# Decay-mask rows inside the exponent matmul of a two-layer SSD, attention and convolution block

## The chip, the core and the metric

The kernel runs on one core of one Trainium2 chip. Its metric is the device time of one execution in microseconds (us), given as the median of several runs. Five engines work side by side, each through its own list of instructions in a fixed order: TensorE (PE in the tables; its weight loads are PEld), VectorE (DVE), ScalarE (ACT), GpSimd (POOL) and SyncE (SP). They wait for one another through semaphores. ScalarE and SyncE also issue most of the DMA transfers; a DMA issue stands in the same list as the engine's other instructions.

## What is computed

Two layers of a hybrid block act on 1024 latent and 256 context tokens (T = 1280, ten chunks of 128 tokens). Each layer projects the tokens, runs three branches (a bidirectional Mamba-2 scan "SSD" with 16 heads, a windowed attention and a convolution), gates them, and projects back. The change is in the SSD branch. Cut to what matters, one direction of it is:

```
da    = dt * a                                   # per head and token
cs    = cumsum(da within a chunk of 128)
seg   = cs[l] - cs[s]
decay = exp(where(s <= l, seg, -inf))            # 128 x 128 per head
y_diag = (C B^T * decay) @ (x * dt)
states, entering states: a scan over the ten chunks
y = y_diag + C @ entering * exp(cs)
```

The backward direction does the same on reversed tokens, so its mask is the other triangle, and the two results are added.

## The kernel before, in words

The layers run one after the other, each as an SSD section, an attention section and an output section. The instruction order of each engine is not the order of the source: a scheduler with a simulated timeline places every instruction, and parts under `high_priority` are drawn ahead. The large projections (`pj`, 512 or 256 columns at a time, three products per weight tile) fill TensorE between the smaller pieces of the SSD.

In the SSD section the prologue forms dt, da, the running sums `cs`, and `ld`, the logarithm of dt. The kernel needs, per chunk and head, exponents of the form log dt[s] - cs[s] + cs[l], and forms them with a matmul on bf16 numbers, where each float32 value is split into three bf16 parts. Lines 739 to 761 prepare this for two groups of 8 heads: VectorE writes the parts of `cs` and `ld` into `qq` (columns 0 to 95) and GpSimd writes -1 into columns 96 to 127; TensorE transposes `qq` chunk by chunk into PSUM tiles `pr`, ScalarE copies them out as `L`, and one DMA per group writes the 48 rows of `cs` parts to DRAM (`csd`).

`half(i)` handles 4 heads over all chunks, 4 times a layer. Line 852: VectorE fills two tiles `R` (128 partitions, 2 directions, 4 heads, 128 tokens) with a pattern of ones that picks the heads. For each chunk, `diag` (lines 867 to 896) then

- issues two DMAs that put `cs` of the chunk into rows 96 to 98 of `R` (line 872),
- forms `pc` with five matmuls: a 128-wide one, two 64-wide ones, and two 64-wide ones against the identity that add the mask `mask_lt` (-3e38 where a triangle is not wanted); and `pd` with four 64-wide ones, two of which add `mask_gt`,
- takes the exponential of both on ScalarE (`ex`, `eb`), adds the two on GpSimd, multiplies by C B^T on VectorE.

There are 40 such decay blocks in layer 0 (ten chunks, four halves) and 32 in layer 1, whose two context chunks need none: 72 in all. What surrounds them is `visit` (the result of a chunk) and the state update `S`. The PSUM tiles of the SSD section, `sm`, `pr`, `pc` and `pd`, share one ring of four banks.

## Time and profile before

| what | value |
|---|---|
| median of 3 runs | 2413.73 us (2412.1 to 2414.97) |
| the profiled execution, its own time | 2409.47 us |
| its span, first to last instruction | 2407.7 us |
| TensorE busy | 96% of the span |
| VectorE, ScalarE, GpSimd busy | 64%, 41%, 45% |
| mean granted TensorE clock | 0.985 of full speed |

The page gives busy times per engine. A matmul's duration is that of its flight, and several fly at once; what a matmul costs on TensorE is read from the distance between the starts of two neighbours.

### The profile page before, as it was taken

The numbers are of one execution on the slowest core, as the hardware profiler recorded it, in microseconds if no ns is written. First come the engines' busy times: TensorE is split into PE (matmuls) and PEld (weight loads), VectorE is DVE, ScalarE is ACT, GpSimd is POOL, SyncE is SP. The second block draws the span as 40 slices with busy tenths as digits, with TensorE's granted clock in tenths as the row PEclk, the third lists the DMA queues.
The fourth block names the chain that finished last, engine by engine and source line by source line (L and its number), as shares of the span: only waits on it lengthen the run. The fifth ranks groups of instructions, "written<-read, shape, count | busy, mean of one in ns | idle before, by whom it ended". The sixth has DMA issues, their size and how long they took to land.

```text
span 2407.7 us, 37133 instructions
## 1 busy us (share of the span) xinstructions
PE 2307.0 (96%) x13453; PEld 1817.5 (75%) x13453; DVE 1533.2 (64%) x2738; ACT 979.0 (41%) x2123; POOL 1085.7 (45%) x1249
## 2 busy tenths in 40 slices
PE   6999999999999999999999999999999999999998
PEld 3787678777877776776888788768768676776798
DVE  4679899941276855865354679979423864865634
ACT  6543243422235454444243443343322355463433
POOL 3237663764453222343233337667575531332333
PEclk8999999999999999999999999999999999999999
DMA  7412212233133112248465311111212312235663
GB/s 225 154 58 87 87 49 64 85 100 111 36 90 105 62 38 70 80 141 264 136 185 168 92 40 45 41 41 43 78 54 62 106 48 67 80 97 171 197 179 107
DMA packets 324248, 237.07 MB, mean 98 GB/s; under 512 B 56066, under 2 KB 280546, under 8 KB 324064
## 3 DMA queue, kind: packets, MB, share of 16 engines
q1 hardware_dynamic: 280832, 193.28, 27.2%
q10 hardware_dynamic: 42336, 41.06, 5.5%
q8 instruction: 106, 1.74, 0.3%
q0 software_dynamic: 896, 0.35, 0.1%
q14 instruction: 78, 0.64, 0.1%
HBM read 181.63 MB, written 53.00 MB: 97 GB/s over the span
## 4 chain that ended last, share of the span: by engine, by line
PE 77%; DVE 9%; DMA 5%; POOL 3%; issue 2%; ACT 2%; SPq 1%; ACTq 0%; DVEq 0%; POOLq 0%
PE pj L96 53%; PE sm L96 6%; PE s L96 4%; PE o L96 3%; PE pt L1086 3%; PE po L96 2%; DVE us L508 2%; DMA raw<-oT 1%; PE pc L96 1%; PE pm L96 1%; DMA wm<-w_mod 1%; POOL ex L893 1%; PE rb L96 1%; DVE acc L596 1%; PE sm L912 1%
## 5 line engine op out<-in xcount | busy, mean ns | idle before, releaser
L96 PE MATMUL pj<-hh,wh 128*128 128x512 f32 (+1 forms) x1840 | 692.7, 377 | 7.8 <-ACT wh L416 2.3
L96 PE MATMUL pj<-hl,wh 128*128 128x512 f32 (+1 forms) x1840 | 686.5, 373 | 1.7 <-POOL hl L199 1.7
L96 PE MATMUL pj<-hh,wl 128*128 128x512 f32 (+1 forms) x1840 | 686.4, 373 | 1.7 <-POOL wl L418 1.6
L418 POOL TENSOR_TENSOR wl<-wr,wh 128x512 fp32r<-128x512 f32 x268 | 362.1, 1354 | 516.8 <-ACT wh L416 482.1
L96 PEld LDWEIGHTS pj<-hh,wh 128*128 128x128 f32 x1840 | 350.0, 190 | 70.7 <-issue 6.8
L96 PEld LDWEIGHTS pj<-hh,wl 128*128 128x128 f32 x1840 | 349.5, 190 | 61.3 <-issue 5.0
L96 PEld LDWEIGHTS pj<-hl,wh 128*128 128x128 f32 x1840 | 350.2, 190 | 59.3 <-issue 5.7
L416 ACT ACTIVATE wh<-wr 128x512 fp32r<-128x512 f32 x344 | 215.6, 630 | 365.5 <-PE pj L96 280.2
L508 DVE SCALAR_TENSOR_TENSOR ua<-gl,vec,ua 128x512 f32<-128x512 f32 (+1 forms) x435 | 303.5, 698 | 12.3 <-ACT ua L506 5.7
L596 DVE SCALAR_TENSOR_TENSOR acc<-raw,vec,acc 128x514 f32<-128x514 f32 (+2 forms) x280 | 191.0, 695 | 21.9 <-ACT acc L593 20.3
L96 PE MATMUL pj<-ho,wh 128*128 128x256 f32 (+1 forms) x896 | 180.3, 300 | 1.0 <-ACT wh L416 1.0
L96 PE MATMUL pj<-hx,wh 128*128 128x512 f32 x512 | 163.7, 400 | 6.9 <-DVE hx L500 2.9
L96 PEld LDWEIGHTS pj<-ho,wh 128*128 128x128 f32 x896 | 145.2, 193 | 6.4 <-ACT wh L416 1.2
L893 POOL TENSOR_TENSOR ex<-ex,eb 64x256 f32<-64x256 f32 x144 | 115.5, 802 | 59.4 <-ACT eb L891 52.4
L933 POOL TENSOR_TENSOR xs<-xk,ws 128x256 f32<-128x256 f32 x144 | 90.7, 641 | 112.0 <-PE sm L96 96.8
L1079 ACT ACTIVATE p<-s,sums 128x512 f32<-128x512 f32 (+1 forms) x144 | 95.5, 663 | 107.7 <-DVE sums L1077 69.4
L1076 DVE TENSOR_REDUCE mx<-s 128x1 f32<-128x512 f32 (+1 forms) x144 | 92.4, 654 | 72.0 <-PE s L96 71.6
L96 PE MATMUL pj<-ho,wl 128*128 128x256 f32 (+1 forms) x448 | 134.6, 301 | 1.1 <-POOL wl L418 0.8
L508 DVE SCALAR_TENSOR_TENSOR us<-gl,vec,us 128x512 f32<-128x512 f32 (+1 forms) x150 | 130.3, 869 | 6.8 <-ACT us L506 4.3
L96 PEld LDWEIGHTS pj<-hx,wh 128*128 128x128 f32 x512 | 97.8, 192 | 30.6 <-DVE hx L500 4.7
L907 POOL TENSOR_TENSOR yp<-yp,ye 128x256 f32<-128x256 f32 x136 | 104.3, 783 | 26.6 <-DVE ye L906 26.1
L1086 PE MATMUL pt<-ident,p 128*128 128x128 f32 x640 | 108.5, 283 | 7.2 <-ACT p L1079 6.5
(325 smaller groups left out, 3951.6 us busy)
## 6 DMA issues: line engine op xcount, KB each, us to landing
wr<-w_in SPq DMA_DIRECT2D x160, 256.0 KB
wr<-w_out SPq DMA_DIRECT2D x114, 256.0 KB
wm<-w_mod SPq DMA_DIRECT2D x64, 256.0 KB
raw<-oT ACTq DMA_DIRECT2D x64, 256.0 KB
wr<-w_out SPq DMA_DIRECT2D x76, 128.0 KB
yT<-yT ACTq DMA_DIRECT2D x72, 128.0 KB
wm<-w_mod SPq DMA_DIRECT2D x16, 512.0 KB
wr<-w_in SPq DMA_DIRECT2D x64, 128.0 KB
```

The lines of the kernel that those rows point to most:

```text
L96: nc.tensor.matmul(o, l, r, start=start, stop=stop)
L416: nc.scalar.activation(out=hi, in_=raw, func=AF.Copy)
L418: low_eng[0].tensor_tensor(out=lo, in0=raw, in1=f32(hi), op=ALU.subtract)
L508: nc.vector.scalar_tensor_tensor(out=u if t == 30 else acc, in0=g[:, t:t + n], scalar=vec2[l][:, t, j:j + 1], in1=acc, op0=ALU.mult, op1=A ...
L596: nc.vector.scalar_tensor_tensor(out=acc, in0=raw[:, i0 + t:i0 + t + n], scalar=v1[:, cw:cw + 1], in1=acc, op0=ALU.mult, op1=ALU.add)
L893: nc.gpsimd.tensor_tensor(out=e[q, :, q], in0=e[q, :, q], in1=eb[q], op=ALU.add)
L907: nc.gpsimd.tensor_tensor(out=y, in0=y, in1=ye, op=ALU.add)
L912: nc.tensor.matmul(ps[:, jj * P:(jj + 1) * P], y[:, jj * P:(jj + 1) * P], ident, start=(jj == 0), stop=False, is_transpose=True)
L933: nc.gpsimd.tensor_tensor(out=h3(xs), in0=xc(c), in1=hb(ws3, c, d), op=ALU.mult)
L1076: nc.vector.tensor_reduce(out=mx, in_=s, axis=mybir.AxisListType.X, op=ALU.min)
L1079: nc.scalar.activation(out=flat(p[:, 0:min(nk, 4), :]), in_=s, func=AF.Exp, scale=-1.0, bias=nm[:, j:j + 1], accum_out=sums[:, 3, j:j + 1])
L1086: nc.tensor.transpose(pt[:, q * P:(q + 1) * P], pr[q][:, i, :], ident)
```

## The change

The masks become part of the matmul that forms the exponents. `L` gets 64 more rows that hold the identity (`id64`), `R` gets 64 more rows that hold the mask, and a third plane, so that one pair of 64-wide matmuls of 512 columns gives all of `pc` and one pair of 256 columns all of `pd`. For the room this takes, `ld` and `cs` are added in float32 before they are split, so `L` needs 48 rows of parts and not 96. The `cs` parts for DRAM get tiles of their own (`qc`, transposed to 72 rows, copied out as `cr`), and `csd` keeps three planes. The constant rows of `R` are written by GpSimd once a layer, and the 48 rows that pick the heads by ScalarE at each half.

```diff
-    csd = [dp.tile([2, 3, 2, 2, 4, T], BF16, ...
+    csd = [dp.tile([2, 3, 2, 3, 4, T], BF16, ...
...
+            nc.vector.tensor_tensor(out=ld, in0=ld, in1=cs, op=ALU.add)
...
             for g in range(2):
+                qc = sp.tile([P, NCH, 72], BF16, tag="xk", name="qc", bufs=7)
+                parts(cs, qc, g)
+                for q, c0 in ((slice(0, 64), 24), (slice(64, P), 0)):
+                    nc.scalar.activation(out=qc[q, :, 48:72], in_=qc[q, :, c0:c0 + 24], func=AF.Copy)
                 qq = sp.tile([P, NCH, P], BF16, tag=("cbs", "btok")[g], name="qq")
-                for c0, t in ((0, cs), (48, ld)):
-                    (four VectorE instructions: three bf16 parts of t)
-                nc.gpsimd.memset(qq[:, :, 96:P], -1.0)
+                parts(ld, qq, g)
+                nc.gpsimd.memset(qq[:, :, 48:64], -1.0)
+                nc.scalar.activation(out=qq[:, :, 64:P], in_=id64 (broadcast), func=AF.Copy)
                 lt = sp.tile([P, T], BF16, tag=f"L{g}", name="L")
                 for b0 in range(0, NCH, 4):
                     nb = min(4, NCH - b0)
                     pr = pp.tile([P, 1024], BF16, tag="sm", name="pr", bufs=NSM)
                     for c in range(b0, b0 + nb):
+                        nc.tensor.transpose(pr[0:72, ...], qc[:, c, :], identb)
+                    cr = sp.tile([72, 512], BF16, tag="ex", name="cr", bufs=2)
+                    nc.scalar.activation(out=cr[:, 0:nb * P], in_=pr[0:72, 0:nb * P], func=AF.Copy)
+                    for v, w in enumerate((0, 2, 1)):
+                        nc.scalar.dma_start(out=csd[l][g][:, :, v]..., in_=cr[24 * w:24 * w + 24, 0:nb * P])
+                    pr = pp.tile([P, 1024], BF16, tag="sm", name="pr", bufs=NSM)
+                    for c in range(b0, b0 + nb):
                         nc.tensor.transpose(pr[...], qq[:, c, :], identb)
                     nc.scalar.activation(out=lt[...], in_=pr[:, 0:nb * P], func=AF.Copy)
-                nc.scalar.dma_start(out=csd[l][g]..., in_=lt[0:48, :])
...
+            for _ in range(2):
+                R = sp.tile([P, 3, 4, P], BF16, tag="R", name="R", bufs=2)
+                nc.gpsimd.memset(R[32:64], 0.0)
+                nc.gpsimd.memset(R[64:P, 0:2], 0.0)
+                for v, t0, m in ((0, 0, mask_lt), (1, 64, mask_lt), (2, 0, mask_gt), (2, 64, mask_gt)):
+                    nc.gpsimd.tensor_copy(out=R[64:P, v, :, t0:t0 + 64], in_=m[64:P, 64:P] (broadcast))
... in half(i):
-                for _ in range(2):
-                    R = sp.tile([P, 2, 4, P], BF16, tag="R", name="R", bufs=2)
-                    nc.vector.tensor_copy(out=R, in_=sel4(sel_c) (broadcast))
+                for R in Rs:
+                    for v, d, t0, t1 in ((0, 0, 0, P), (2, 1, 0, P), (1, 1, 0, 64), (1, 0, 64, P)):
+                        nc.scalar.activation(out=R[0:48, v, :, t0:t1], in_=sel_c[0:48, d, ...] (broadcast), func=AF.Copy)
... in diag(c):
-                    for dd in range(2):
-                        nc.scalar.dma_start(out=R[96:99, dd], in_=csd[l][g, :, dd, hf, :, c * P:(c + 1) * P])
+                    nc.scalar.dma_start(out=R[48:51], in_=csd[l][g, :, hf, :, :, c * P:(c + 1) * P])
-                    mm(pc[:, :, qs[1]], lt[0:99, c * P:(c + 1) * P], r0[:, :, qs[1]], start=True, stop=False)
-                    mm(pc[qs[0], :, qs[0]], ll[0], r0[:, :, qs[0]], start=False, stop=False)
-                    mm(pc[qs[1], :, qs[0]], ll[1], r1[:, :, qs[0]], start=False, stop=False)
-                    for q in qs:
-                        mm(pc[q, :, q], identb[:, q], mask_lt (broadcast), start=False, stop=True)
+                    for v, (q, lq) in enumerate(zip(qs, ll)):
+                        mm(pc[q], lq, R[:, v])
...
                     for q, lq in zip(qs, ll):
-                        mm(pc[q], lq, r1[:, :, q], start=True, stop=False)
-                    for q in qs:
-                        mm(pc[q], identb[:, q], mask_gt (broadcast), start=False, stop=True)
+                        mm(pc[q], lq, R[:, 2, :, q])
```

How this moves instructions. On TensorE, at the first decay block of layer 0, the order before was (`sm<-S,ct` and `sm<-xs,btok` are the state products ahead of it; a pair is two matmuls of 64 output rows, `64x4x64` means 64 rows and 256 columns):

```order
L96 MATMUL sm<-S,ct 128x256 x2
L96 MATMUL sm<-xs,btok 128x256 x2
L96 LDWEIGHTS L
L96 MATMUL pc<-R,L 128x4x64
L96 LDWEIGHTS L
L96 MATMUL pc<-R,L 64x4x64
L96 LDWEIGHTS L
L96 MATMUL pc<-R,L 64x4x64
L96 LDWEIGHTS identb
L96 MATMUL pc<-mask_lt,identb 64x4x64
```

On TensorE, at the same place, the order now is the whole block and the projection behind it:

```order
L96 MATMUL sm<-S,ct 128x256 x2
L96 MATMUL sm<-xs,btok 128x256 x2
L96 LDWEIGHTS L
L96 MATMUL pc<-R,L 64x512
L96 LDWEIGHTS L
L96 MATMUL pc<-R,L 64x512
L96 LDWEIGHTS L
L96 MATMUL pd<-R,L 64x4x64
L96 LDWEIGHTS L
L96 MATMUL pd<-R,L 64x4x64
L96 MATMUL pj<-hh_982,wl 128x512
```

Nine matmuls with nine weight loads (a mask matmul and four of `pd` follow the piece above) have become four with four.

On ScalarE, in the set-up of layer 0 where `L` is copied out of PSUM, the order before was (L760 writes `cs` to DRAM, L872 loads it into `R`, `btok` is the next user of the PSUM ring):

```order
L759 ACTIVATE L<-pr 128x512 x2
L759 ACTIVATE L<-pr 128x256
L759 ACTIVATE L<-pr 128x512
L760 DMA cs_104<-L 48x1280
L872 DMA R<-cs_104 3x4x128 x4
L759 ACTIVATE L<-pr 128x512
L759 ACTIVATE L<-pr 128x256
L814 ACTIVATE btok<-sm 128x512
```

On ScalarE, at the same place, the order now is (L772 copies `cr`, L778 `L`, L774 writes to DRAM, L894 loads `R`):

```order
L778 ACTIVATE L<-pr 128x512
L774 DMA cs_107<-cr 6x4x512 x5
L894 DMA R<-cs_107 3x12x128 x2
L774 DMA cs_107<-cr 6x4x512
L772 ACTIVATE cr<-pr 72x256
L778 ACTIVATE L<-pr 128x256
L778 ACTIVATE L<-pr 128x512
L774 DMA cs_107<-cr 6x4x256 x3
L772 ACTIVATE cr<-pr 72x512
L778 ACTIVATE L<-pr 128x512
L774 DMA cs_107<-cr 6x4x512 x3
L772 ACTIVATE cr<-pr 72x512
```

The load of `R`, which waits for a write to DRAM, now stands ahead of two thirds of the copies out of the PSUM ring, and more writes stand between these; `btok` comes after two more rows.

On ScalarE, at the end of the second half in layer 0, the order now is (L902 and L907 are the exponentials `ex` and `eb` of the last blocks, L876 the refill of `R` for the next half, L932 and L933 the result of a chunk):

```order
L876 ACTIVATE R<-sel_c 48x512
L902 ACTIVATE ex<-pc 128x512
L933 DMA yT_105<-yT 128x2x128
L876 ACTIVATE R<-sel_c 48x4x64 x2
L932 ACTIVATE yT<-sm 128x256
L907 ACTIVATE eb<-pd 128x256
L876 ACTIVATE R<-sel_c 48x512
L894 DMA R<-cs_107 3x12x128
```

The refill stands between the exponentials of the last blocks; before, none of it was on ScalarE.

## Rows read from the trace of the kernel before

**Rows 1.** The page, busy time, share of the span and instructions of each engine.

```profile
PE 2307.0 (96%) x13453; PEld 1817.5 (75%) x13453; DVE 1533.2 (64%) x2738; ACT 979.0 (41%) x2123; POOL 1085.7 (45%) x1249
```

**Rows 2.** Windows: stretch, length, busy us (count) per engine, granted clock, DMA, GB/s.

```profile
120.00:580.00 460.00, 448.77 (x2867) 347.28 (x2866) 357.61 (x635) 163.25 (x345) 275.55 (x400) 1.00 0.26 76
1560.00:1600.00 40.00, 32.45 (x211) 22.27 (x210) 34.64 (x59) 14.57 (x32) 34.15 (x47) 0.96 0.12 35
1600.00:1785.00 185.00, 185.00 (x997) 147.89 (x994) 104.63 (x165) 58.59 (x119) 115.51 (x165) 1.00 0.22 58
1785.00:1807.00 22.00, 16.51 (x143) 10.06 (x141) 8.63 (x17) 7.78 (x20) 16.56 (x22) 1.00 0.16 44
```

**Rows 3.** Timeline of PE over one decay block: start, length, line, operation, count.

```profile
177.82 0.42 PE L912 MATMUL sm<-ident,yp 128*128 128x128 f32 x2
178.08 0.51 PE L96 MATMUL pc<-R,L 99*128 99x256 bf16 x3
178.41 0.28 PE L96 MATMUL pc<-mask_lt,identb 128*64 128x256 bf16 x2
178.53 0.28 PE L96 MATMUL pd<-R,L 99*64 99x256 bf16 x2
178.64 0.28 PE L96 MATMUL pd<-mask_gt,identb 128*64 128x256 bf16 x2
178.85 0.33 PE L912 MATMUL sm<-ident,yp 128*128 128x128 f32 x1
```

**Rows 4.** Timeline of the weight loads over the same block.

```profile
178.31 0.11 PEld L96 LDWEIGHTS <-identb 128*64 128x64 bf16 x2
```

**Rows 5.** Timeline of PE, a block with projections between `pc` and `pd`.

```profile
335.69 0.28 PE L96 MATMUL pc<-mask_lt,identb 128*64 128x256 bf16 x2
335.89 0.50 PE L96 MATMUL pj<-hh,wh 128*128 128x512 f32 x1
336.23 0.39 PE L96 MATMUL pj<-hl,wh 128*128 128x512 f32 x1
336.46 0.40 PE L96 MATMUL pj<-hh,wl 128*128 128x512 f32 x1
```

**Rows 6.** Timeline of PE in the set-up of layer 0.

```profile
149.31 0.95 PE L758 MATMUL pr<-identb,qq 128*128 128x128 bf16 x14
150.09 0.50 PE L96 MATMUL pj<-hh,wh 128*128 128x512 f32 x1
...
155.09 1.04 PE L813 MATMUL sm<-ident,raw 128*128 128x128 f32 x8
```

**Rows 7.** Timeline of ACT there; ACTq is its queue issuing DMAs.

```profile
149.93 1.85 ACT L759 ACTIVATE L<-pr 128x512 bf16<-128x512 bf16 x4
151.32 0.36 ACTq L760 DMA_DIRECT2D cs<-L  x1
153.38 1.43 ACTq L872 DMA_DIRECT2D R<-cs  x4
...
155.94 0.60 ACT L814 ACTIVATE btok<-sm 128x512 f32<-128x512 f32 x1
```

**Rows 8.** Timeline of DVE there, two rows of the splitting of `cs`.

```profile
144.04 0.31 DVE L737 TENSOR_SCALAR cs<-cs 128x320 f32<-128x320 f32 x1
...
148.94 0.55 DVE L751 TENSOR_TENSOR qq<-cs,qq 128x160 bf16<-128x160 f32 x2
```

**Rows 9.** Group of line 852 by form: busy us, mean ns, idle before.

```profile
L852 DVE COPY R<-sel_c 128x1024 bf16<-128x1024 bf16 x16 | 14.2, 895 | 3.6 <-PE pd L96 3.4
```

**Rows 10.** The instructions of line 759, durations in ns min/median/max.

```profile
L759 ACT ACTIVATE L<-pr x12: 378/594/628, 149.9 to 1413.2; 128x512 bf16<-128x512 bf16 x8, 128x256 bf16<-128x256 bf16 x4
```

**Rows 11.** Timeline of POOL at the start of layer 0's SSD section.

```profile
62.68 0.66 POOL L752 MEMSET qq<- 128x320 bf16 x2
67.07 1.30 POOL L418 TENSOR_TENSOR wl<-wr,wh 128x512 fp32r<-128x512 f32 x1 [3.72 <-ACT wh L416]
86.22 1.27 POOL L199 TENSOR_TENSOR hl<-xs,hh 128x512 fp32r<-128x512 f32 x1 [17.85 <-ACT xs L198]
```

**Rows 12.** Timeline of PE, first use of that `wl`.

```profile
73.20 0.28 PE L96 MATMUL pj<-hh,wl 128*128 128x256 f32 x1
```

More of the change, by code (lines that the diff above doesn't have):

```diff
@@ L119, in build @@
     nc.vector.tensor_scalar(out=mask_gt, in0=tril, scalar1=-1.0, scalar2=-NEG, op0=ALU.add, op1=ALU.mult)
-    sel_c = cp.tile([P, 16], BF16, name="sel_c")
+    sel_c = cp.tile([P, 2, 8], BF16, name="sel_c")
     sel4 = cp.tile([P, 32], F32, name="sel4")
-    nc.vector.tensor_reduce(out=sel4[:, 0:16], in_=ident[:, 0:96].rearrange("p (a b) -> p b a", b=16), axis=mybir.AxisListType.X, op=ALU.add)
-    nc.vector.tensor_copy(out=sel_c, in_=sel4[:, 0:16])
+    for d in range(2):
+        nc.vector.tensor_reduce(out=sel4[:, 8 * d:8 * d + 8], in_=ident[:, 24 * d:24 * d + 24].rearrange("p (a b) -> p b a", b=8), axis=mybir.AxisListType.X, op=ALU.add)
+    nc.vector.tensor_copy(out=sel_c, in_=sel4[:, 0:16].rearrange("p (a b) -> p a b", b=8))
+    id64 = cp.tile([P, 64], BF16, name="id64")
+    nc.vector.tensor_tensor(out=id64, in0=identb[:, 0:64], in1=identb[:, 64:P], op=ALU.add)
     nc.vector.tensor_reduce(out=sel4, in_=ident.rearrange("p (a b) -> p b a", b=32), axis=mybir.AxisListType.X, op=ALU.add)
@@ L138, in build @@
     yTd = [dp.tile([P, KD, T], F32, name=f"yT{l}") for l in range(DEPTH)]
-    csd = [dp.tile([2, 3, 2, 2, 4, T], BF16, name=f"cs{l}") for l in range(DEPTH)]
+    csd = [dp.tile([2, 3, 2, 3, 4, T], BF16, name=f"cs{l}") for l in range(DEPTH)]
     glTd = [dp.tile([P, 4, RA], F32, name=f"glT{l}") for l in range(DEPTH)]
@@ L737, in ssd_section, with v4, parts @@
             nc.vector.tensor_scalar_mul(out=cs, in0=cs, scalar1=-1.0)
+            nc.vector.tensor_tensor(out=ld, in0=ld, in1=cs, op=ALU.add)
             L = []
+            def v4(ap):
+                return ap.rearrange("p c (d j) -> p c d j", d=2)
+            def parts(t, q, g):
+                x = v4(v3(t))[:, :, :, 8 * g:8 * g + 8]
+                q = [q[:, :, 0:48].rearrange("p c (d a j) -> p c d a j", d=2, a=3)[:, :, :, k, :] for k in range(3)]
+                nc.vector.tensor_copy(out=q[0], in_=x)
+                nc.vector.tensor_tensor(out=x, in0=x, in1=q[0], op=ALU.subtract)
+                nc.vector.tensor_copy(out=q[1], in_=x)
+                nc.vector.tensor_tensor(out=q[2], in0=x, in1=q[1], op=ALU.subtract)
             for g in range(2):
+                qc = sp.tile([P, NCH, 72], BF16, tag="xk", name="qc", bufs=7)
+                parts(cs, qc, g)
+                for q, c0 in ((slice(0, 64), 24), (slice(64, P), 0)):
+                    nc.scalar.activation(out=qc[q, :, 48:72], in_=qc[q, :, c0:c0 + 24], func=AF.Copy)
                 qq = sp.tile([P, NCH, P], BF16, tag=("cbs", "btok")[g], name="qq")
-                def v4(ap):
-                    return ap.rearrange("p c (d j) -> p c d j", d=2)
-                for c0, t in ((0, cs), (48, ld)):
-                    x = v4(v3(t))[:, :, :, 8 * g:8 * g + 8]
-                    q = [v4(qq[:, :, c0 + 16 * k:c0 + 16 * k + 16]) for k in range(3)]
-                    nc.vector.tensor_copy(out=q[0], in_=x)
-                    nc.vector.tensor_tensor(out=x, in0=x, in1=q[0], op=ALU.subtract)
-                    nc.vector.tensor_copy(out=q[1], in_=x)
-                    nc.vector.tensor_tensor(out=q[2], in0=x, in1=q[1], op=ALU.subtract)
-                nc.gpsimd.memset(qq[:, :, 96:P], -1.0)
+                parts(ld, qq, g)
+                nc.gpsimd.memset(qq[:, :, 48:64], -1.0)
+                nc.scalar.activation(out=qq[:, :, 64:P], in_=id64.unsqueeze(1).to_broadcast([P, NCH, 64]), func=AF.Copy)
                 lt = sp.tile([P, T], BF16, tag=f"L{g}", name="L")
@@ L845, in half @@
                 lt = L[g]
[L847 to L853 removed]
+                for R in Rs:
+                    for v, d, t0, t1 in ((0, 0, 0, P), (2, 1, 0, P), (1, 1, 0, 64), (1, 0, 64, P)):
+                        nc.scalar.activation(out=R[0:48, v, :, t0:t1], in_=sel_c[0:48, d, 4 * hf:4 * hf + 4].unsqueeze(2).to_broadcast([48, 4, t1 - t0]), func=AF.Copy)
                 def xc(c):
@@ L870, in diag @@
                     nv[0] += 1
[L871 to L874 removed]
+                    nc.scalar.dma_start(out=R[48:51], in_=csd[l][g, :, hf, :, :, c * P:(c + 1) * P])
                     qs = [slice(0, 64), slice(64, P)]
[L876 removed]
+                    ll = [lt[:, c * P + a:c * P + a + 64] for a in (0, 64)]
                     pc = pp.tile([P, 4, P], F32, tag="sm", name="pc", bufs=NSM)
[L878 to L882 removed]
+                    for v, (q, lq) in enumerate(zip(qs, ll)):
+                        mm(pc[q], lq, R[:, v])
                     e = sp.tile([P, 4, P], F32, tag="ex", name="ex", bufs=2)
@@ L886, in diag @@
                     for q, lq in zip(qs, ll):
-                        mm(pc[q], lq, r1[:, :, q], start=True, stop=False)
-                    for q in qs:
-                        mm(pc[q], identb[:, q], mask_gt[:, q].unsqueeze(1).to_broadcast([P, 4, 64]), start=False, stop=True)
+                        mm(pc[q], lq, R[:, 2, :, q])
                     eb = sp.tile([P, 4, 64], F32, tag="eb", name="eb", bufs=2)
```

14 lines of the change are left out of this document (5 added, 9 removed).

## Prediction

> **What bounds the kernel now.** I read four views in turn. The page's busy line [rows 1] shows TensorE busy for 96% of the span and no other engine above 64%. The table of windows [rows 2] tells where that is strict: in 120 to 580 us TensorE is busy 448.77 of 460 and in 1600 to 1785 all of 185, at a granted clock of 1.00, while VectorE, GpSimd and ScalarE idle for much of the time. In 1560 to 1600 and in 1785 to 1807 TensorE is busy only 32.45 of 40 and 16.51 of 22, and VectorE (34.64) or GpSimd (34.15, 16.56) is as busy as TensorE: there the chain through the engines sets the time. So time taken from TensorE counts in full in the dense stretches, and work given to another engine costs only where TensorE ends up waiting for it. The timeline of single instructions then prices one decay block [rows 3, 5] and the set-up of the exponents [rows 6 to 8, 11, 12].
>
> A matmul's length in the timeline is its flight; its cost is the distance to the next start.
>
> **The decay block.** Before, a block runs from 178.08 to 178.85, 0.77 us [rows 3]. It is five slots of 256 columns (the 128-wide matmul; the 64-wide pair; the mask pair; the `pd` pair; its mask pair), since two 64-wide matmuls lie side by side in one slot. A slot is 0.115: 178.41, 178.53, 178.64. Five are 0.57, and I put the other 0.20 down to two changes between full-width and half-width matmuls, 0.10 each. Now there is a pair of 512 columns and a pair of 256. A start-to-start of 512 columns is 0.23 (336.23 to 336.46, [rows 5]), so 0.23 + 0.115 + 0.20 = 0.545. That is 0.225 less, and for 72 blocks 16.2 us. Besides, one half-width run now replaces a full-width matmul between half-width ones; counted through TensorE's order, changes beside blocks fall from 209 to 175, 34 x 0.10 = 3.4 (the 0.20 from the last mask pair to the next full-width matmul in [rows 5], less 0.115, shows one). Gross gain 19.6.
>
> Bounds of this: if the 512-column pairs take two slots each way (no side by side), nothing is gained; if the changes cost nothing now, 0.10 x 2 x 72 = 14 more. I take the middle, since pairs of 256 columns do lie side by side.
>
> 14 of the 72 blocks lie in the two chained stretches. Their share, 14 x (19.6 / 72) = 3.8, I count a third: +2.5 (bounds 0 and 3.8).
>
> One point on the weights. The load for the second half-width pair, 0.11 long, starts at 178.31 while the `pc` matmuls are still in flight, and the pairs behind it follow 0.115 apart [rows 3, 4]: loads are hidden, and I take nothing for them. The Trainium skill (TensorE: Matmul & The Clock Gate, The mechanism, under packing small matmuls) says that a weight load overlaps matmuls in flight only when its rows of the array differ; the two pairs share their rows, so by it the loads would be exposed, and the trace of before disagrees.
>
> **The set-up, TensorE.** The parts of `cs` are now transposed by themselves: 40 more transposes. Fourteen take 149.31 to 150.09, 0.056 each [rows 6]: +2.2, in full, as TensorE is dense there.
>
> **The set-up, ScalarE.** This is the term with the widest bounds. ScalarE takes its list in order. A load of `R` waits for the write of `cs` to land in DRAM: before, the write is issued at 151.32 for 0.36 and the load starts at 153.38, about 1.7 after the issue's end [rows 7]. In the new order the load stands ahead of two thirds of the copies that empty the PSUM ring. Ahead of `btok` (155.94 in [rows 7]) I count: five copies `cr` at 1.85 / 4 = 0.46, 2.3; eleven more issues at 0.36, 3.9, less 0.7 for two loads of `R` fewer; about 1 where `cr`, with two buffers, waits for its own writes. That is some 6.5 later. TensorE shares the ring of four banks and stalls when it isn't emptied; behind it lie only the transposes `btok` (155.09, [rows 6]). It has 1.1 of the added transposes there to do and I allow 1 of slack, leaving 4. VectorE splits `ld` only after adding `cs`: one add of about 0.31 (as at 144.04, [rows 8]) and the splits of `ld`, now behind those of `cs`, where the last rows ended at 148.94 + 0.55; ScalarE's small copies inside `qc` and of the identity into `qq` stand there too. For this +1. In all +5 for layer 0, bounds 0 (other projections are drawn in) and 8 (everything shows). Layer 1 has more projection matmuls between these transposes, by its order: +1, bounds 0 and 5.
>
> **The refill of R.** VectorE loses 16 fills of 895 ns, 14.2 us [rows 9]; TensorE hardly waits for VectorE in the dense stretches (357.61 of 460, [rows 2]), so 0, with a bound of -3 in the chained ones. ScalarE gets 16 x (2 x 0.594 + 2 x 0.378) = 16 x 1.94 = 31.1 us, by the copies of 512 and 256 columns [rows 10]. ScalarE is busy 163.25 of 460 [rows 2], so it has room, but in a list with fixed order: at each of the six boundaries between halves 3.9 us stand between the exponentials of the last blocks. TensorE has projections to go on with; I take 0.25 a boundary, +1.5 (bounds 0 and 6 x 3.9 = 23). The Trainium skill (ScalarE: Activation LUTs, Rules for kernel authors) wants simple operations on VectorE and not ScalarE, up to about three times as fast in bf16. The rows agree in direction (895 ns for 1024 columns against twice 594 and more), with 14.2 against 31.1 us; on a ScalarE that isn't the bound it makes no time by itself. DMA issues on ScalarE: loads of `R` fall from 144 to 72, writes of `cs` rise from 4 to 36; the loads stand in the dense part, so the exchange favours the blocks slightly, and I take 0.
>
> **GpSimd.** It writes the constant rows of `R` once a layer: per tile memsets of 1536 and 1024 columns, at 0.66 for 640 [rows 11] 2.64, and for both tiles eight copies of 256 that I put at 0.4 each: 8.5 in all with both tiles (bounds 7.3 and 11.7, at 0.26 and 0.8 a copy). Most of it stands ahead of `wl` at 67.07, which has 3.72 idle before it: it comes about 3.9 late (3.3 to 6.7), and is ready near 72.3 for its first use at 73.20 [rows 12]. So 0, bound +2. After it GpSimd has 17.85 idle before 86.22 [rows 11] to catch up.
>
> **The sum.** -19.6 + 2.5 + 2.2 + 5 + 1 + 1.5 = -7.4. The profiled execution's own time is 2409.47, so 2402.1 on its footing; the median of the runs shown is 4.26 above it, and the forecast is 2406.3, put as 2406.
>
> **Rivals.**
>
> A, everything beside the blocks is hidden. TensorE's own balance, -19.6 + 2.2 = -17.4, arrives: 2413.7 - 17.4 = 2396. For it: ScalarE at 35% in the dense stretch, and projections that can be drawn into the set-up. Against: 14 blocks in chained stretches, and the load of `R` placed ahead of the copies.
>
> B, the weights pace the new block. Four loads of 0.11 stand against three slots of 0.115, where before nine stood against five; if those of the `pd` pair can't go while the `pc` pair is in flight, each block pays 0.11, 72 x 0.11 = 7.9: 2406.3 + 7.9 = 2414. Against it is the load at 178.31 [rows 4], which did overlap; for it, that load was of `identb`, and no row shows one of `L` at such a moment. The section of the skill named above is this rival's rule.
>
> C, ScalarE becomes the late engine. If the refills come when the exponentials that release the ring's banks are due, two thirds of 23.3, 15.5, show in place of 1.5: -7.4 - 1.5 + 15.5 = +6.6, 2420. It is slower than before once some 9 of the 23.3 show. For it: one ring of four banks for `pc`, `pd`, `sm` and `pr`, so one late exponential stops TensorE. Against: ScalarE's 300 us idle in 460.
>
> D, the change doesn't do what it says: half-width matmuls of 512 columns don't lie side by side. Then the `pc` pair takes 0.46, 0.23 x 72 = 16.6 more: 2423. Nothing in the rows hints at it but that no half-width pair of 512 is among them.
>
> **How the numbers follow.** A difference under 0.2%, 4.8 us, can't be told from none. Chances: forecast 0.55, A 0.15, B 0.17, C 0.10, D 0.03. Within the forecast the set-up (0 to 8, 0 to 5) and the chained blocks spread it over 2399 to 2412; four fifths of that lies below 2408.9. Faster: 0.44 + 0.15 = 0.59; within: 0.11 + 0.17 = 0.28; slower: 0.13. The range 2394 to 2418 leaves out C and D and a tail of A, under 2 in 10.
>
> **What would show it.** In the profile after: a block's first start to the next full-width start of 0.55, and not 0.66 (B) or 0.77 (D); the start after a 512-column pair 0.23 later. TensorE's busy time lower by about 17, with its idle time in layer 0's set-up higher by some 5: transposes `btok` around 160 less what was saved before them, and a load of `R` in ScalarE's list with idle time before it. Refills between exponentials, with `pc` matmuls waiting for ScalarE by at most a few tenths at a boundary; several us there would be C. `wl` near 71 and its use still at 73. The forecast is wrong if TensorE's idle time grows by more than 17, or if the blocks don't shrink.

## The result and the profile after

The change made the kernel slower. Its median is 2429.86 us (2427.79 to 2434.31), that of the kernel before on the same chip 2414.35 (2412.10 to 2415.70); the ratio is 1.0068, with a 95% interval of 1.0052 to 1.0085. The forecast was 2406, range 2394 to 2418. The profiled execution has a span of 2429.9 us.

The line of busy times, which answers to [rows 1], shows that TensorE is busy for as long as before (2307.0), in a span that is 22 us longer. It has less to do but does it at a lower clock: the mean granted clock is 0.979, where it was 0.985, which leaves out 51 us of full-speed clock instead of 36. Its idle time has grown from 100.7 to 123.1 us.

```profile
PE 2306.8 (95%) x13133; PEld 1812.6 (75%) x13133; DVE 1520.5 (63%) x2726; ACT 1013.5 (42%) x2211; POOL 1091.9 (45%) x1273
```

The span is best cut at points that both kernels pass, at the same projection matmul by count: the set-up of the exponents in layer 0, the rest of layer 0's SSD section with its 40 blocks, and the SSD section of layer 1. The windows of the kernel before (stretch, length, busy us and count of TensorE, its weight loads, VectorE, ScalarE, GpSimd, granted clock, DMA share, GB/s):

```profile
130.90:162.94 32.04, 31.00 (x225) 26.30 (x224) 20.34 (x50) 19.26 (x40) 4.14 (x10) 1.00 0.19 58
162.94:632.21 469.27, 454.08 (x2835) 350.80 (x2834) 341.17 (x595) 154.93 (x326) 285.15 (x402) 0.99 0.28 79
1341.82:1837.93 496.11, 477.57 (x2647) 380.33 (x2646) 354.93 (x588) 184.39 (x366) 291.05 (x402) 0.99 0.19 52
```

and of the changed kernel, from and to the same matmuls:

```profile
135.86:178.02 42.16, 35.26 (x239) 29.02 (x237) 18.64 (x49) 22.40 (x48) 3.23 (x8) 0.92 0.15 47
178.02:640.72 462.70, 444.88 (x2642) 340.33 (x2639) 335.43 (x591) 164.60 (x354) 283.60 (x403) 0.99 0.28 81
1349.28:1859.35 510.07, 480.34 (x2508) 381.60 (x2506) 352.29 (x581) 200.47 (x410) 292.46 (x415) 0.97 0.19 51
```

The set-up takes 10.1 us longer: TensorE idles for 6.9 us where it idled for 1.0, and its clock, which was at the upper of its two levels all through (1.00 is 2.4 GHz), has a mean of 0.92, which over 42.16 us is 3.4 us lost. Layer 0's blocks win 6.6 and layer 1's section loses 14.0. The rest is +5.0 ahead of the set-up (+1.5 in another profile of almost the same program, n2 below, so mostly not the change), -1.0 between the layers and about +1 behind.

The decay block became what the forecast said. The timeline of TensorE at one block, to be held against [rows 3, 5]:

```profile
353.64 0.41 PE L96 MATMUL pc<-R,L 128*64 128x512 bf16 x2
353.88 0.28 PE L96 MATMUL pd<-R,L 128*64 128x256 bf16 x2
354.08 0.50 PE L96 MATMUL pj<-hh,wh 128*128 128x512 f32 x1
354.42 0.39 PE L96 MATMUL pj<-hl,wh 128*128 128x512 f32 x1
```

The 512-column pair lies side by side (0.24 to the next start) and the `pd` pair adds 0.20 with the change of width: 0.44 from the first start to the next full-width start, where it had been 0.77. The other change of width, which lay inside the old block, now lies ahead of it: from the last `sm<-ident,yp` to the block it is 0.20 (median of 11 blocks without a wait) where it was 0.11 (13 blocks). That makes 0.54 in all. The 0.34 behind the block's end is no new cost, since a full-width matmul behind a mask pair showed it too (335.89 to 336.23, [rows 5]). No start is held up by a weight load's 0.11 [rows 4].

The timeline of ScalarE in layer 0's set-up, to be held against [rows 7] (ACTq: its queue issuing DMAs; in brackets idle time and what ended it):

```profile
157.38 1.31 ACTq L774 DMA_DIRECT2D cs<-cr  x1
157.72 0.60 ACT L772 ACTIVATE cr<-pr 72x512 bf16<-72x512 bf16 x1
158.20 0.60 ACT L778 ACTIVATE L<-pr 128x512 bf16<-128x512 bf16 x1
158.73 3.03 ACTq L774 DMA_DIRECT2D cs<-cr  x4
161.94 0.68 ACTq L894 DMA_DIRECT2D R<-cs  x2
162.65 0.71 ACTq L774 DMA_DIRECT2D cs<-cr  x1
163.41 0.38 ACT L772 ACTIVATE cr<-pr 72x256 bf16<-72x256 bf16 x1 [4.61 <-DMA cs<-cr]
163.69 0.37 ACT L778 ACTIVATE L<-pr 128x256 bf16<-128x256 bf16 x1
163.82 0.71 ACTq L774 DMA_DIRECT2D cs<-cr  x1
163.96 0.59 ACT L778 ACTIVATE L<-pr 128x512 bf16<-128x512 bf16 x1
164.57 1.46 ACTq L774 DMA_DIRECT2D cs<-cr  x2
166.15 0.59 ACT L772 ACTIVATE cr<-pr 72x512 bf16<-72x512 bf16 x1 [1.60 <-issue]
166.65 0.58 ACT L778 ACTIVATE L<-pr 128x512 bf16<-128x512 bf16 x1
166.78 2.21 ACTq L774 DMA_DIRECT2D cs<-cr  x3
169.11 0.59 ACT L772 ACTIVATE cr<-pr 72x512 bf16<-72x512 bf16 x1 [1.88 <-issue]
169.61 0.37 ACT L778 ACTIVATE L<-pr 128x256 bf16<-128x256 bf16 x1
169.74 0.71 ACTq L774 DMA_DIRECT2D cs<-cr  x1
169.87 0.59 ACT L841 ACTIVATE btok<-sm 128x512 f32<-128x512 f32 x1
```

A write of `cs` holds ScalarE's list for 0.71 to 0.76 us (3.03 for four; thirteen of them stand ahead of `btok`), twice the 0.36 of [rows 7], and ScalarE copies nothing out of the ring between 158.8 and 163.4 and little until 169.9. The 4.61 us ahead of the copy at 163.41 are filled by seven issues; between the end of the four writes issued in a row (161.76) and the load of `R` (161.94) there is no room for a wait of more than 0.18. TensorE, which has four banks to transpose into, waits. Its longest waits in the set-up, in its own timeline:

```profile
155.46 0.41 PE L770 MATMUL pr<-identb,qc 128*72 128x128 bf16 x4 [1.73 <-ACT qc L760]
163.84 0.38 PE L770 MATMUL pr<-identb,qc 128*72 128x128 bf16 x4 [0.38 <-ACT cr L772]
166.80 0.37 PE L777 MATMUL pr<-identb,qq 128*128 128x128 bf16 x2 [1.93 <-ACT cr L772]
169.76 1.54 PE L840 MATMUL sm<-ident,raw 128*128 128x128 f32 x6 [1.36 <-ACT cr L772]
```

So 3.7 of its 6.9 idle us are waits for the late copies `cr`, and 1.7 one for ScalarE's small copies inside `qc`. With e1 (below) the three waits for `cr` are gone.

GpSimd's constant rows behaved as costed against [rows 11, 12]: the `wl` behind them starts at 71.23 (forecast "near 71") and no TensorE wait hangs on it:

```profile
71.23 1.29 POOL L422 TENSOR_TENSOR wl<-wr,wh 128x512 fp32r<-128x512 f32 x1
```

The refill is 30.8 us of ScalarE, by the groups of its line (31.1 forecast):

```profile
L876 ACT ACTIVATE R<-sel_c 48x512 bf16<-48x512 bf16 x32 | 19.2, 623 | 13.6 <-PE pc L96 12.3 <-POOL R L784 1.3
L876 ACT ACTIVATE R<-sel_c 48x256 bf16<-48x256 bf16 x32 | 11.6, 408 | 0.0
```

### The profile page after: what moved, and what is told of

Read it like the earlier page. It is cut to its first block, busy times and chain, and to the rows that moved or that the text cites. A ratio compares the mean times of both kernels' runs of the same rounds, so it can differ in the third digit from the quotient of the medians.

```text
span 2429.9 us, 36533 instructions
## 1 busy us (share of the span) xinstructions
PE 2306.8 (95%) x13133; PEld 1812.6 (75%) x13133; DVE 1520.5 (63%) x2726; ACT 1013.5 (42%) x2211; POOL 1091.9 (45%) x1273
```

## The experiments

Eighteen kernels were run. Ratios are to the kernel before, run in the same sessions, with 95% intervals; 0.1% is 2.4 us. "Set-up", "layer 0" and "layer 1" are the three windows above, found in each profile by the same matmuls. Since a profile is a single execution, a difference in a window is relied on only where several kernels repeat it. The profiled executions of the kernel before (2409.5 us), of b1 (2401.1) and of e8 (2420.7) lie 4 us or more under the median of their kernel, those of b2 (2410.9) and e7 (2406.7) 4 us or more above theirs.

| kernel | ratio | set-up | layer 0 | layer 1 |
|---|---|---|---|---|
| before | 1 | 32.0 | 469.3 | 496.1 |
| changed | 1.0068 [1.0052, 1.0085] | 42.2 | 462.7 | 510.1 |
| e1 writes on SyncE | 1.0036 [1.0025, 1.0047] | 38.2 | 466.8 | 505.3 |
| e2 fill on VectorE | 1.0041 [1.0027, 1.0056] | 43.7 | 467.5 | 508.6 |
| e4 both | 1.0025 [1.0014, 1.0035] | 38.0 | 463.3 | 506.3 |
| e5 and first loads on SyncE | 0.9994 [0.9985, 1.0004] | 37.4 | 465.1 | 507.8 |
| e6 and one transpose | 0.9992 [0.9980, 1.0003] | 36.7 | 466.7 | 500.4 |
| e7 and refill by DMA | 0.9935 [0.9920, 0.9950] | 36.1 | 455.8 | 501.1 |
| e8 changed, refill by DMA | 1.0048 [1.0035, 1.0061] | 43.5 | 456.7 | 507.1 |
| e3 changed, masks' time again | 1.0084 [1.0069, 1.0099] | 42.2 | 465.2 | 506.7 |
| e9 e7, masks' time again | 1.0016 [1.0007, 1.0025] | 36.8 | 463.0 | 501.0 |
| b2 before, no masks | 0.9959 [0.9945, 0.9973] | 32.1 | 462.0 | 501.4 |
| b1 before, fill on ScalarE | 0.9973 [0.9962, 0.9985] | 31.9 | 464.6 | 497.0 |
| b3 before, refill by DMA | 1.0015 [1.0006, 1.0023] | 31.9 | 469.3 | 501.3 |
| n1 before, other order | 1.0021 [1.0012, 1.0030] | 32.7 | 472.7 | 500.3 |
| n2 changed, other order | 1.0060 [1.0045, 1.0074] | 43.0 | 462.3 | 506.2 |
| n4 e6, other order | 0.9994 [0.9985, 1.0003] | 36.7 | 462.9 | 502.4 |
| n3 e7, other order | 1.0010 [1.0001, 1.0019] | 36.1 | 460.2 | 499.3 |
| n5 e7, nearly the same order | 0.9968 [0.9957, 0.9980] | 36.1 | 455.8 | 498.5 |
| n6 b2, other order | 0.9978 [0.9969, 0.9987] | 32.7 | 460.4 | 501.8 |

**ScalarE's list in the set-up: e1, e2, e4, e5.**

```diff
-  nc.scalar.dma_start(out=csd[l][g][:, :, v]..., in_=cr[24 * w:24 * w + 24, ...])
+  nc.sync.dma_start(out=csd[l][g][:, :, v]..., in_=cr[24 * w:24 * w + 24, ...])      # e1, e4, e5
-  nc.scalar.activation(out=R[0:48, v, :, t0:t1], in_=sel_c..., func=AF.Copy)
+  nc.vector.tensor_copy(out=R[0:48, v, :, t0:t1], in_=sel_c...)                      # e2, e4, e5
-  nc.scalar.dma_start(out=R[48:51], in_=csd[l][g, :, hf, :, :, ...])
+  (nc.sync if i == 0 and nv[0] <= 2 else nc.scalar).dma_start(out=R[48:51], ...)     # e5
```

Expected of e1: 

> The changed kernel with one difference: the writes of the cs parts to DRAM are issued by SyncE and not by ScalarE. In the changed kernel each of them takes 0.71 us in ScalarE's list (the forecast had 0.36), and TensorE lost 10.1 us to the kernel before between 131 and 163 us, and 2.6 in layer 1's set-up. Theory 1 (ScalarE's list holds up the set-up): these two stretches win back most of it, 8 to 12 us, so about 2419. Theory 2 (ScalarE's list is not what holds TensorE there; the transposes and the wait for the write to land are): within 3 us of the changed kernel's 2430. Theory 3 (the order that the scheduler lays out anew costs, whatever the edit): any sign, and the gain or loss not in these stretches.

Expected of e2: 

> The changed kernel with one difference: the 48 rows of R are filled by VectorE, as in the kernel before, and not by ScalarE. Theory 1 (the refill between exponentials on ScalarE holds TensorE at the six half boundaries, where the changed kernel loses some 2 to 7 us each to the kernel before): about 12 us faster than the changed kernel, 2418. Theory 2 (the boundaries are late for another reason, GpSimd or the new order): within 3 us of 2430. Theory 3 (VectorE is the worse place, since the chained stretches of layer 1 are bound by it): slower than 2430.

Expected of e4: 

> The changed kernel with both: the cs writes issued by SyncE and the 48 rows of R filled by VectorE. Theory 1 (ScalarE's list is what ate the gain): the two differences add up, 20 to 24 us faster than the changed kernel, 2406 to 2410, at or under the kernel before. Theory 2 (each only moves the wait to another engine): no better than the better of the two alone. Theory 3 (the new order costs by itself): 2420 or more.

Expected of e5: 

> The kernel with both earlier differences (cs writes issued by SyncE, R filled by VectorE; 2421 us) and one more: the first two loads of cs into R in each layer are issued by SyncE too, so that ScalarE's list has no load that waits for the writes to land while it has to empty the PSUM ring. In that kernel ScalarE copies nothing between 154.9 and 159.6 us, and the first decay block stands 7.1 us later than in the kernel before. Theory 1 (that wait holds the set-up): 3 to 5 us faster, 2416 to 2418, with the first block of layer 0 at 178 to 180 instead of 182.5. Theory 2 (what is left of the set-up's delay is the added transposes and copies themselves): within 2 us of 2421.

e1 went from 1.0068 to 1.0036 with intervals apart, 7.7 us, and its set-up is 4 us shorter, at every measurement of a kernel with the writes on SyncE (38.2 us and less against 42.2 and more): theory 1 of e1, a little under its size. e2 is 1.0041, with an interval that touches the changed kernel's; its set-up is no shorter and its half boundaries are not better (layer 0's window grew), so it does not show that the fill mattered. e4 is no clear step from e1. e5 is: 1.0025 to 0.9994, 7.5 us, intervals apart. What it removed can be read in e4's timeline of ScalarE,

```profile
154.32 0.60 ACT L778 ACTIVATE L<-pr 128x512 bf16<-128x512 bf16 x1
157.12 0.98 ACTq L894 DMA_DIRECT2D R<-cs  x2
159.57 0.38 ACT L772 ACTIVATE cr<-pr 72x256 bf16<-72x256 bf16 x1 [4.65 <-DMA R<-cs]
```

where the load waits for the write to land, from 154.92 to 157.12, and the next copy starts 4.65 us after the copy before it. In e5 ScalarE's list has no such load, and the same copy waits for TensorE:

```profile
157.00 0.38 ACT L772 ACTIVATE cr<-pr 72x256 bf16<-72x256 bf16 x1 [3.14 <-PE pr L770]
```

It still waits 3.14 us, so the load's own share of the 4.65 is some 1.5. The window of the set-up shrank by 0.6, and the first block came at 180.8 and not 182.5. Of the 7.5 us most are outside that window: in the two profiles 6.5 lie between the layers (703.65 against 710.12), where the edit itself changes nothing and where the other kernels take 706.5 to 714.5. So e5's step is not shown to be the load's. What is shown is that the three edits together bring the changed kernel level with the kernel before.

**What a shorter block is worth: e3, b2.** e3 and b2 are mirror images: the masks' time put back into the changed kernel, and taken out of the kernel before.

```diff
+  for q in qs:                                                                       # e3 (and e9)
+      mm(pc[q, :, q], identb[:, q], zero.unsqueeze(2).to_broadcast([P, 4, 64]), start=False, stop=True)
...
-  for q in qs:                                                                       # b2 (and n6)
-      mm(pc[q, :, q], identb[:, q], mask_lt[:, q]..., start=False, stop=True)
-  nc.scalar.activation(out=flat(e), in_=flat(pc), func=AF.Exp)
+  nc.scalar.activation(out=flat(e), in_=flat(pc), func=AF.Exp, scale=0.001)
```

Expected of e3: 

> The changed kernel with four more matmuls in each block, pairs of 256 columns against zeros in the places of the old mask matmuls, so that TensorE's block costs again about what it cost before; results are unchanged by them. Theory 1 (the shorter block reached the end of the kernel and was outweighed by other losses): slower than the changed kernel by 0.225 us for each of the 58 blocks outside the chained stretches and a third of that in the others, 14 us or more, 2444. Theory 2 (the block's gain never reached the end, since TensorE waits for other engines behind it): within 4 us of 2430.

Expected of b2: 

> The kernel before with the four mask matmuls of each block left out (and the exponents scaled by 0.001 so that nothing overflows; the masks are then not applied). Its set-up, its refill and its other engines' work are as before, and a block has three slots where it had five, 0.23 us less, 72 times. Theory 1 (TensorE's time in a block arrives in full at the end, and all that went wrong in the changed kernel is set-up and refill): 14 to 17 us faster than the kernel before, 2397 to 2400. Theory 2 (about half of it arrives, as when the masks' time was given back to the changed kernel, which cost 8 where 16 were put in): 2405 to 2408. Theory 3 (nothing arrives): 2414.

b2 removes two slots of 0.115 from 72 blocks, 16.6 us, with the set-up untouched; it is 0.41% faster, 9.9 us, nearest to theory 2 (its median is 2406.77). The windows say which part arrived. Those of b2, and the stretch of layer 1 in which it differs most, first b2's and then the row of the kernel before for the same 20 us (b2's layer 1 starts 5.7 us earlier; the row of the kernel before shifted by these 5.7 reads 19.47 us busy and a clock of 1.00):

```profile
162.88:624.89 462.01, 442.69 (x2674) 342.40 (x2673) 344.87 (x595) 153.93 (x326) 281.24 (x402) 1.00 0.29 81
1336.12:1837.56 501.44, 477.05 (x2520) 380.40 (x2518) 356.14 (x588) 183.81 (x366) 289.56 (x402) 0.97 0.19 52
...
1500.00:1520.00 20.00, 16.69 (x110) 12.51 (x110) 17.54 (x26) 6.24 (x16) 9.27 (x11) 0.85 0.13 35
```

```profile
1500.00:1520.00 20.00, 20.00 (x138) 14.11 (x137) 16.02 (x26) 5.96 (x13) 9.72 (x15) 1.00 0.17 48
```

In layer 0, 40 blocks by 0.23 are 9.2 and the window is 7.3 shorter: most of it arrived. In layer 1, 32 blocks are 7.4 and the window is 5.3 longer. These two profiled executions differ from their medians in opposite directions, so the pair n1 and n6 (below: the kernel before and b2, each with the same added copies) is the better witness. Its windows of layers 0 and 1, first n1's, then n6's:

```profile
163.04:635.70 472.66, 454.82 (x2835) 349.83 (x2833) 339.71 (x595) 154.95 (x329) 283.69 (x402) 0.99 0.28 79
1346.37:1846.62 500.25, 481.64 (x2648) 382.61 (x2647) 356.89 (x588) 185.46 (x370) 285.87 (x402) 0.98 0.20 52
162.19:622.59 460.40, 443.93 (x2675) 343.24 (x2673) 344.29 (x595) 154.64 (x329) 281.06 (x402) 0.99 0.29 81
1333.72:1835.50 501.78, 477.82 (x2519) 381.28 (x2518) 356.53 (x588) 184.85 (x370) 288.79 (x402) 0.97 0.20 52
```

Layer 0 wins 12.3 and layer 1 loses 1.5. Both pairs agree that layer 0 gets the gain and layer 1 nothing of it. In the stretch shown, TensorE of the kernel before was full; with less to do there it waits (3.3 us idle in b2), and its clock is 0.85 and not 1.00. b2's wait in that stretch, in the timeline of TensorE:

```profile
1515.96 0.69 PE L908 MATMUL sm<-ident,yp 128*128 128x128 f32 x2 [2.82 <-POOL yp L903]
```

Over the whole window of layer 1, TensorE idles 24.4 us in b2 and 24.0 in n6, at a mean clock of 0.97; in the four kernels with masks (before, n1, b1, b3) it idles 18.5 to 20.8, at 0.98 or 0.99. The mean clock of whole executions, over all of a kernel's runs, is 0.9838 in the kernel before as run beside b2 and 0.9820 in b2, 0.9835 in n1 and 0.9808 in n6. Of 2415 us that is 4 to 7 us of full-speed clock, the size of what is missing between 16.6 and 10. So in layer 1, where TensorE waits for results of GpSimd and VectorE as soon as it has less to do, time taken from it did not come back as time.

e3 came out at 1.0084 against 1.0068, with overlapping intervals: 4 us (8 by the medians), less than theory 1's 14. Its layer 0 lost 2.5 and its layer 1 gained 3.4 on the changed kernel, and its mean clock over all runs is higher, 0.982 against 0.979. This agrees with b2 in kind: what is given or taken on TensorE in layer 1 does not show.

**The doubled transposes: e6.**

```diff
-  qc = sp.tile([P, NCH, 72], ...);  qq = sp.tile([P, NCH, P], ...)     # two transposes a chunk
+  parts(cs, qq, g, 48); (72 columns with the swapped copy); parts(ld, qq, g, 0)
+  nc.gpsimd.tensor_copy(out=lt[64:P]..., in_=identb[64:P, 64:P]...); nc.gpsimd.memset(lt[32:64], -1.0)
+  nc.scalar.activation(out=lt[0:48, ...], in_=pr[0:48, ...], func=AF.Copy)
+  nc.vector.tensor_copy(out=cr[0:120, ...], in_=pr[0:120, ...])
```

Expected of e6: 

> As the one before, and the set-up has one transpose for each chunk and group again (20 a layer, not 40): the parts of ld (48 columns) and of cs (72) share a tile; the rows of -1 and of the identity are written into L once a layer by GpSimd and are not transposed; ScalarE copies 48 rows to L, VectorE the rest to cr. Theory 1 (the doubled transposes and copies through the ring of four banks hold the set-up): 3 to 5 us faster than with 40 transposes, 2412 to 2415, first block of layer 0 within 2 us of 175.4. Theory 2 (the longer chain on VectorE, or the later write and load, hold it): no gain by it.

No difference in time (0.9992 and 0.9994), as theory 2 had it. The windows moved, however: with one transpose layer 1 takes 498.5 to 502.4 in six kernels, with two 505.3 to 510.1 in eight. What that layer gained is missing between the layers, where e6 takes the usual 710.8 and e5's profile the unusual 703.65. Its set-up, 36.7, is still 4.6 above the kernel before, and its timeline of TensorE names one more cause:

```profile
150.06 0.95 PE L770 MATMUL pr<-identb,qq 128*128 128x128 bf16 x14 [2.12 <-DVE qq L764]
```

TensorE waits 2.1 us for VectorE's splits, which now include `ld` behind `cs`.

**The refill: e7, e8, b1, b3.** e7 and e8 bring the 48 rows of `R` at a half by DMA from a copy in DRAM, e7 on top of e6, e8 in the changed kernel; b3 does the same in the kernel before, and b1 moves its fill to ScalarE.

```diff
-  for R in Rs: (four copies of sel_c into R[0:48])
+  if i:                                                                # e7, e8; b3 alike
+      for R in Rs:
+          nc.scalar.dma_start(out=R[0:48], in_=seld[hf])
...
-  nc.vector.tensor_copy(out=R, in_=sel4(sel_c)...)                     # b1
+  for d in range(2): nc.scalar.activation(out=R[:, d], in_=sel4(sel_c)[:, d]..., func=AF.Copy)
```

Expected of e7: 

> As the one before, and the 48 rows of R that pick the heads are refilled at the halves by one DMA each from a copy in DRAM, made once, so that neither ScalarE nor VectorE spends time on it. Theory 1 (the refill costs at the boundaries whichever engine does it): 2 to 4 us faster than with VectorE's refill. Theory 2 (VectorE's refill is hidden, or the time for the DMA to land takes its place): within 2 us.

Expected of e8: 

> The changed kernel with one difference: from the second half of a layer on, the 48 rows of R come by one DMA each from a copy in DRAM, and no engine computes them; the set-up of the exponents is left as the change made it. Theory 1 (the refill is the largest single loss, and moving it from ScalarE to VectorE, which won 3 us, only moved it): 12 to 16 us faster than the changed kernel, 2414 to 2418. Theory 2 (its gain of 16 us came only because the set-up had been mended first): 3 to 5 us, 2425 to 2427.

Expected of b3: 

> The kernel before with one difference: from the second half of a layer on, R is refilled by one DMA each from a copy in DRAM and not by VectorE. Theory 1 (the kernel before hides its fill, one VectorE instruction of 0.9 us for each R; the loss belongs to the changed kernel's four copies): within 3 us of the kernel before. Theory 2 (a fill by an engine costs at the boundaries in either kernel, so that the gain of 16 us is one that the kernel before could have had without the change): 8 us or more faster.

Expected of b1: 

> The kernel before with one difference: the fill of R is done by ScalarE, two copies of 512 columns for each R, in place of VectorE's one. Theory 1 (a fill that stands between the exponentials on ScalarE holds the decay blocks at the boundaries): 4 to 12 us slower than the kernel before. Theory 2 (the place of the fill does not matter): within 3 us.

e7 is the fastest kernel of the study, 2400.51 us, 0.65% under the kernel before. But e8 won only 0.20% on the changed kernel (intervals overlap), b3 lost 0.15%, and b1, which should have lost, won 0.27%. No theory about the fill gives all four. Layer 0's window does give one thing four times: with the DMA it takes 455.8, 456.7, 460.2 and 455.8 us (e7, e8, n3, n5), with four copies on an engine 462.3 to 467.5 in eight kernels. The row of e8, to be held against the changed kernel's 462.70:

```profile
175.97:632.62 456.65, 442.72 (x2634) 339.93 (x2633) 339.11 (x590) 154.47 (x327) 282.69 (x403) 0.99 0.29 84
```

So the refill costs layer 0's window some 6 us, and without it the window is 12.6 under the kernel before: the block's gain is all there. Over the whole kernel e8 shows 4.8 us, with overlapping intervals. The kernel before, with one instruction for each `R`, gains nothing there by the DMA (469.3 both times).

**The order by itself: e9, n1 to n6.** Each edit lets the scheduler lay out another order. In the kernels n1 to n6 nothing is added but one copy of 4 columns a half:

```diff
+  nc.scalar.activation(out=nudge, in_=xk[4][:, 0, 0:4], func=AF.Copy)  # n1, n2, n4, n5, n6; on VectorE in n3
```

Expected of e9: 

> The fastest kernel so far (cs writes and first loads on SyncE, one transpose for each chunk and group, R refilled by DMA) with four matmuls of 256 columns against zeros put back in each block, so that a block costs TensorE about what it cost before the change. Theory 1 (with refill and set-up out of the way a block's time arrives in full): 14 to 17 us slower than without them, 2415 to 2418. Theory 2 (in layer 1 the time freed in a block turns into waiting and a lower clock, and about half arrives): 7 to 10 us slower, 2408 to 2411.

Expected of n1: 

> The kernel before with one copy of 4 columns added on ScalarE in each half, whose result nobody reads; by it the scheduler lays out another order (562 rows of TensorE's list differ). Theory 1 (what the edits changed is what they cost): within 2 us of the kernel before. Theory 2 (the order alone moves the time): 3 to 8 us from it, either way.

Expected of n2: 

> The changed kernel with the same copy of 4 columns in each half (487 rows of TensorE's list differ). Theory 1: within 2 us of the changed kernel's 2430. Theory 2 (the order alone moves the time): 3 to 8 us from it, either way; but still slower than the kernel before, since the set-up's 10 us do not hang on the order.

Expected of n3: 

> The fastest kernel so far (2400.5, refill by DMA) with a copy of 4 columns in each half, on VectorE (some 400 rows of TensorE's list differ). Theory 1 (the gain of 16 us is the refill's): within 2 us of 2400. Theory 2 (much of the gain was a lucky order): 2405 to 2412.

Expected of n4: 

> The kernel with one transpose for each chunk and VectorE's refill (2416) with the copy of 4 columns on ScalarE in each half (377 rows of TensorE's list differ). Theory 1: within 2 us of 2416. Theory 2 (the order alone moves the time): 3 to 10 us from it, and if faster, the refill by DMA is worth that much less than 16.

Expected of n5: 

> The fastest kernel (2400.5) with the copy of 4 columns in each half on ScalarE and not on VectorE; so placed it leaves the order nearly as it was (9 rows of TensorE's list differ, where 422 did with the copy on VectorE, 2418 us). Theory 1 (the order made the 17 us): within 4 us of 2400. Theory 2 (the added copies, or the fastest kernel's measurement, made them): 2410 or more.

Expected of n6: 

> The kernel before without the four mask matmuls of a block (exponents scaled by 0.001, masks not applied; 2407) with the copy of 4 columns on ScalarE in each half, by which 248 rows of TensorE's list differ. Theory 1 (a block shorter by 0.23 us is worth about 10 us whatever the order): 2409 to 2413, 8 to 12 under the kernel before with the same copy (2421). Theory 2 (its 10 us were the order's): 2415 or more.

n1 made the kernel before 0.21% slower, 5 us; n2 and n4 changed nothing; n3 made e7 0.75% slower, 18 us, and n5, whose order is e7's but for a few rows, 0.33%, 8 us. That is theory 2 of n5 (2409.98 us): the added copies, or e7's measurement with six runs, account for 8. n3 and n5, with the same number of copies, differ by 0.42%, 10 us; so the order (with the engine of the copy) is worth up to 5 us at n1 and some 10 at e7. Of e7's 16 us over e6, some 6 are left in n5 and none in n3. Why n5 loses 8 with hardly another order is open (its profiled execution takes 2406.6 us, e7's 2406.7, and their windows are alike). e9 loses 0.81% to e7, 0.48% to n5 and 0.06% to n3, so it cannot say what the masks' time costs. n6 can, since it has the same copies as n1: 0.9978 against 1.0021, 10.4 us, as b2 against the kernel before (9.9). A block shorter by 0.23 us is worth 10 us in the kernel before, in two orders.

## Why the prediction was wrong

**The block, -19.6.** The size on TensorE was right (0.54 against 0.545 and 0.77), though the sign named for it, 0.55 from the first start to the next full-width start, came out as 0.44, since one change of width moved ahead of the first start. What the block is worth at the end was wrong: b2 and n6 give 10 us for 16.6. The step that failed is "14 of the 72 blocks lie in the two chained stretches", with a part of their gain struck off and the gain of the other 58 counted in full. In layer 0 the gain arrives (n6 12.3 under n1, e8 12.6 under the kernel before). Of the 18 blocks of layer 1 that were counted in full, nothing shows: n6 takes 1.5 more there than n1, b2 5.3 more than the kernel before, and the changed kernels with 20 transposes (498.5 to 502.4) as much as the kernels with masks (496.1 to 501.3). Layer 1's section as a whole behaves as the chained stretches do: with the masks gone TensorE waits in places where it had been full, as in b2 at 1500 to 1520. And I gave such waits no price for the clock, which was lower there. By two of its own signs the forecast was wrong as well: TensorE's busy time is not lower by 17 but the same, and its idle time grew by 22.

**The set-up, +5 with bounds 0 and 8.** With the 1.1 of layer 0's added transposes the forecast is 6.1. It is 10.1, and 10.1 to 11.7 in the five kernels that keep it as the change made it. The term that was mis-sized is "eleven more issues at 0.36": an issue of this shape takes 0.71 us (36 of them), and 13 stand ahead of `btok`; the writes on SyncE take 4 us off. The wait of the load, 1.7 before, adds next to nothing in the changed kernel, since the issues ahead of it take longer (0.18 at most), and some 1.5 in e4. The splits and small copies, "+1", show as 1.7 in the wait for `qc`, and as 2.1 in e6. Not in the sum at all: the clock, 1.00 before and 0.92 now, 3.4 us.

**The set-up of layer 1, +1.** Kernels with 40 transposes a layer take some 6 us more in layer 1 than those with 20. It begins at the set-up: the first exponential `ex` of layer 1 starts 137.9 us into the window in the kernel before (138.3 to 139.5 in b1, b2, b3, n1 and n6), 143.0 to 143.2 in the six with 20 transposes and 149.0 to 153.3 in the eight with 40. TensorE fills most of that delay with projections: its waits in the first 160 us are 3.4 to 4.7 us with 20 transposes and 4.9 to 7.3 with 40. Which later waits make the 6 us is open.

**The refill, +1.5 with bounds 0 and 23.** Some 6 us in layer 0 by e8, with the engine that does it of little matter: e2's move to VectorE, [rows 9] against [rows 10], did not win it back. The term was too small, within its bounds. Rival C, ScalarE as the late engine, was the right neighbourhood (2420 forecast for it), but it named the refill, which gave 4.8 us when taken off ScalarE (e8), and the writes of `cs` gave 7.7 (e1).

**GpSimd, 0, and the weights, 0** held: `wl` is in time, and the block's starts leave no room for an exposed load, so rivals B and D are out. The rule of the Trainium skill behind B (TensorE: Matmul & The Clock Gate, The mechanism), that a load overlaps matmuls in flight only where its rows differ, would have made the `pd` pair start 0.35 after the `pc` pair (0.24 and the load's 0.11); it starts 0.24 after it, and the measurement decides.

**The balance.** By windows: set-up +10.1, layer 0 -6.6, layer 1 +14.0, the rest about +5, 22 us in the profiled execution; by the medians 16. In layer 1's 14, the profiled execution of the kernel before was a good one: n1, b1 and b3, which do the same work, take 497.0 to 501.3. Against these the loss is 9 to 13, and 5 to 9 in n2's order of the changed kernel; 6 go with the doubled transposes, and what is left, refill and order among it, is not divided further. The 7.4 us that the shorter blocks should have given there, and did not, come on top as missing gain.

**The outcome.** With writes, first loads and fill moved off ScalarE's list the change comes out level, with two transposes or with one (e5; e6, n4: 0.9992 to 0.9994). With the refill by DMA as well it is 0.65% faster, 0.32% faster or 0.10% slower in three kernels of the same work but for a few tiny copies (e7, n5, n3). e7 beats both kernels as measured; that the change then helps whatever the order is not shown.

## What to carry to other kernels

Price a DMA issue by its own shape and look at what stands behind it in the issuing engine's list: here the engine that had to empty the PSUM ring spent 4.6 us on seven issues. Time taken from a busy engine was worth its full size in layer 0 and nothing in layer 1, where the next engines were close behind; so test such a gain by leaving the work out before rebuilding anything around it, as b2 did in one edit, and look at the clock besides the idle time. And where a scheduler lays out the order anew, time the same work in two or three orders before giving a few us to an edit.

## What was not expected of the hardware

A write of 24 rows of 1 KB or half a KB to DRAM, in pieces of four rows, took 0.71 us of ScalarE's list (median of 36 issues, 0.70 to 1.31), one of 48 rows of 2.5 KB 0.32 to 0.37, a load of 9 KB 0.24 to 0.35. In b2's 20 us with 3.3 us of idle time on TensorE the mean granted clock was 0.85, and 110 matmuls were done where the kernel before did 138; n6 repeats it (0.83 and 104 matmuls in 1500 to 1520). Over the whole kernel, leaving out 16.6 us of matmuls went with a mean clock lower by 0.002 to 0.003 in both pairs.
